# Input product of a recurrent layer in pairs of channel tiles by seven products, on one Trainium2 core

## The chip, the cores and the metric

The kernel runs on one core of one Trainium2 chip, as one program for the whole model. The metric is device time in microseconds (us) for one execution. Its engines are TensorE (PE; PEld is its weight load), VectorE (DVE), ScalarE (ACT), GpSimd (POOL) and SyncE (SP), which issues most DMAs.

## The reference

One sequence of 1024 tokens, model width 1024, two layers, fp32. Layer 0 mixes by retention and a gated delta rule, layer 1 by a gated linear recurrence (RG-LRU); each is followed by a feed-forward block with a short convolution (inner width 2816). The change is about the recurrent mixer of layer 1 and what stands just ahead of it.

```python
h = h + conv_ffn(rms_norm(h, norm_ffn[0]), ...)        # layer 0's feed-forward block
hn = rms_norm(h, norm_mix[1])
h = h + rglru_mixer(hn, ...)                            # layer 1
h = h + conv_ffn(rms_norm(h, norm_ffn[1]), ...)
return rms_norm(h, norm_final)

def rglru_mixer(hn, w_in, conv_w, conv_b, w_a, b_a, w_x, b_x, lam, w_out):
    gate, xr = jnp.split(hn @ w_in, 2, axis=-1)         # w_in: 1024 x 2048, "the input product"
    xr = causal_dwconv(xr, conv_w) + conv_b             # 4 taps along the tokens
    xb = xr.reshape(b, t, 8, 128)                       # 8 channel blocks
    r = sigmoid(einsum('btni,nij->btnj', xb, w_a) + b_a)
    i = sigmoid(einsum('btni,nij->btnj', xb, w_x) + b_x)
    log_a = -8.0 * r * softplus(-lam)
    a = exp(log_a)
    u = sqrt(-expm1(2.0 * log_a)) * (i * xr)
    hs = scan over tokens of hs[t] = a[t] * hs[t-1] + u[t]
    return (gelu(gate) * hs) @ w_out                    # "the output product"

def conv_ffn(hn, w_up, conv_w, conv_b, w_down):
    gate, val = split(causal_dwconv(hn @ w_up, conv_w) + conv_b)
    return (silu(gate) * val) @ w_down
```

## The kernel before, in words

**Layout.** Channels lie on the 128 partitions, the 1024 tokens along the free axis, in two halves of 512. The residual stream is eight tiles `H[0..7]` of 128x1024. A product of fp32 quality is three fp32r matmuls (`mm3`, L313 to L315): each operand is split in a high part, rounded by a ScalarE copy, and a low part, the rest, by a VectorE subtraction; high x high, high x low and low x high are added in PSUM.

**Weights** stream from DRAM in quarters of 128x512: SP issues the load into one of seven buffers `raw`, ScalarE casts `whi` (L267), VectorE makes `wlo` (L268). The order of all quarters is written out in `quarter_order`, and `prefetch` issues loads and splits six quarters (`RING`) ahead of the one in use, so that these steps stand between others in ScalarE's and VectorE's order. Engines work in program order each; outside blocks marked `manual_schedule` a scheduler may still move instructions at build time.

**The feed-forward blocks** take their products in *pairs*: two channel tiles (one of the gate, one of the value) are a 2x2 block problem in output tiles and token columns, done by seven products `o` = 0 to 6 in place of eight (`pair_products`). Each product is 4 x 3 matmuls of 128x512. The seven operands are sums and differences of quarters of the normed input, built once (`operand_steps`: scale, `normal`, `sub`, `high`, `low`) and kept in `s1` and `s2`; the seven weight sums are made by VectorE in `load_pair`. The results need sums too (`pair_sums`): ScalarE copies products 0, 1 and 2 from PSUM into buffers `kept`, VectorE adds products 3 to 5 to these into the two buffers `halo`, ScalarE copies product 6 there. PSUM banks are shared by the string `BANK`: products with the same letter accumulate onto one another.

```python
BANK = "ACACABA"
```

So product 2 adds onto the bank in which product 0 stood, product 3 onto that of product 1, and so on: the next product may begin in a bank when the copy or sum that reads the one before has been done.

The operands for the *second* feed-forward block are built beside matmuls that are going on: those of the first token half (`pair_operands`) while the output product of the recurrent layer is at its second half (called from `down_pairs`), those of the second (`late_operands`) inside `pair_halves`, which does the first pair of products in token halves, with VectorE's and ScalarE's order written out.

**The recurrent layer** does not do this. `down_x`, the end of layer 0's feed-forward block, adds each product to `H` and splits the scaled result for both halves into 32 slots of `s1` (`norm_step`, L383 and L384); the norm factor, one per token, is a row `R` that is multiplied in behind each product. Then eight steps: `proj_x` (one channel tile of the x half: 2 token halves x 8 x 3 matmuls, evacuated by VectorE, L373), `stage_x` (convolution, L1051 and L1053, and the split into `xs`, L586 and L587), `stage_g` for the tile before (12 + 12 matmuls with the two gate matrices into PSUM tiles `pc`, then on ScalarE tanh L1070, exp L1075, tanh L1076, square root L1082, between VectorE's products L1081, L1083, L1084 and the scan L1085), and `stage_y` for the tile before that (the gate half of the input product, L1094, GELU on ScalarE, L1095, product with the scan, L1096, store to `y_dram`). The gates' temporaries are eight 128x512 buffers `us`. A change of function on ScalarE between tanh or exp, square root and GELU shows as an ACT_TABLE_LOAD.

After the last step the y tiles are loaded back and split, and `down_pairs(ys, "lru_out", gain)` does the output product, adds it to `H` and builds the next operands.

## Time and profile before

| | |
|---|---|
| time, median of 3 runs | 2153.62 us (2153.57 to 2155.07) |
| the profiled execution: its time / its span | 2152.99 us / 2151.2 us |
| granted TensorE clock | 0.999 |
| PE busy | 2137.9 us, 99% of the span, 10716 matmuls |
| DVE busy | 1693.5 us, 79% |
| ACT busy | 1082.8 us, 50% |
| POOL busy | 98.2 us, 5% |

The span is the time from the first to the last instruction in the trace; an execution's own time is 1.8 us longer. The recurrent layer stands from about 1206 to 1412 us of the span, its output product behind that. The profile below writes groups of instructions as "line, engine, operation, out<-in by the program's names, partitions x elements, count | busy us, mean ns | idle before, and what ended it", and a timeline as "start, length (both us), engine, line, operation". A timeline row with "x2" holds two instructions one behind the other. An instruction's length includes its start and end latency, so neighbours overlap: the distance between two starts (the pitch) is what one more costs its engine. The column of the granted clock (PEclk) is 1.00 at full speed.

### The profile page before, as it was taken

What the parts mean: (1) busy time and instruction counts of PE and PEld (TensorE: products, weight loads), DVE (VectorE), ACT (ScalarE), POOL (GpSimd) and SP (SyncE); (2) the same over time, 40 slices, a digit from 0 to 9 for tenths busy, and PEclk for the clock granted to TensorE, in tenths of its full rate; (3) what the DMA queues carried; (4) which work ended last, traced back from release to release, by engine and by line L of the source; (5) the groups of instructions that cost most, each with busy time, mean ns of one, the idle gap of its engine ahead of it and who ended that gap; (6) DMA issues with size and microseconds to landing.
All of it is one profiled execution on the core that took longest, in us unless ns stands there. A gap on an engine that the chain in (4) does not pass through costs nothing.

```text
span 2151.2 us, 29709 instructions
## 1 busy us (share of the span) xinstructions
PE 2137.9 (99%) x10716; PEld 1783.3 (83%) x10716; DVE 1693.5 (79%) x2565; ACT 1082.8 (50%) x1748; POOL 98.2 (5%) x114
## 2 busy tenths in 40 slices
PE   9999999999999999999999999999999999999998
PEld 7877889888888888888888888888888888888887
DVE  7995676656999889888866787778999889888645
ACT  6444433235665555555324476756655555554321
POOL 0102022300000000000000000000000000000001
PEclk9999999999999999999999999999999999999999
DMA  5354423444145445437636312242354345375542
GB/s 187 92 168 127 134 89 96 166 128 131 55 155 174 146 158 191 156 109 273 230 104 205 87 54 80 70 154 68 119 180 167 143 159 178 118 266 178 181 169 84
DMA packets 205171, 307.98 MB, mean 143 GB/s; under 512 B 29376, under 2 KB 92384, under 8 KB 205024
## 3 DMA queue, kind: packets, MB, share of 16 engines
q1 hardware_dynamic: 197760, 299.60, 41.9%
q10 hardware_dynamic: 6240, 5.97, 0.9%
q8 instruction: 84, 1.38, 0.3%
q0 software_dynamic: 1024, 0.53, 0.1%
q14 instruction: 63, 0.52, 0.1%
HBM read 215.27 MB, written 90.74 MB: 142 GB/s over the span
## 4 chain that ended last, share of the span: by engine, by line
PE 93%; DVE 3%; DMA 1%; issue 1%; SPq 0%; ACT 0%; POOL 0%; POOLq 0%; DVEq 0%; ACTq 0%
PE ps L313 28%; PE ps L314 28%; PE ps L315 28%; PE pc L313 1%; PE pc L314 1%; PE pc L315 1%; DVE l L1333 0%; DVE l L1331 0%; PE pc L483 0%; DMA l<-gc_dram 0%; DVE wlo L268 0%; PE ps L1508 0%; PE pc L1464 0%; PE ps L1606 0%; PE pc L1576 0%
## 5 line engine op out<-in xcount | busy, mean ns | idle before, releaser
L313 PE MATMUL ps<-s,whi 128*128 128x512 f32 (+1 forms) x2704 | 1054.5, 391 | 1.1 <-ACT s L383 0.7
L314 PE MATMUL ps<-s,whi 128*128 128x512 f32 (+1 forms) x2704 | 1047.9, 388 | 0.5 <-DVE s L900 0.5
L315 PE MATMUL ps<-s,wlo 128*128 128x512 f32 (+1 forms) x2704 | 1047.3, 388 | 0.0
L267 ACT CAST whi<-raw 128x512 fp32r<-128x512 f32 (+1 forms) x620 | 376.6, 613 | 628.4 <-PE ps L314 494.6
L313 PEld LDWEIGHTS ps<-s,whi 128*128 128x128 f32 x2704 | 507.8, 188 | 106.6 <-ACT s L383 1.3
L315 PEld LDWEIGHTS ps<-s,wlo 128*128 128x128 f32 x2704 | 507.7, 188 | 104.7 <-DVE wlo L268 0.6
L314 PEld LDWEIGHTS ps<-s,whi 128*128 128x128 f32 x2704 | 508.1, 188 | 102.5 <-DVE s L900 1.9
L268 DVE TENSOR_TENSOR wlo<-raw,whi 128x512 fp32r<-128x512 f32 (+1 forms) x620 | 415.7, 676 | 72.0 <-ACT whi L267 60.8
L828 DVE SCALAR_TENSOR_TENSOR t<-halo,cols,t 128x1024 f32<-128x1024 f32 x176 | 221.6, 1281 | 2.6 <-ACT t L826 1.6
L801 DVE TENSOR_TENSOR halo<-ps,kept 128x512 f32<-128x512 f32 (+1 forms) x138 | 91.8, 666 | 74.4 <-PE ps L315 73.2
L811 DVE TENSOR_TENSOR h<-ps,h 128x512 f32<-128x512 f32 x112 | 77.3, 690 | 78.8 <-PE ps L315 78.8
L826 ACT ACTIVATE t<-halo,cols 128x1024 f32<-128x1024 f32 x88 | 109.5, 1246 | 18.6 <-DVE halo L801 10.2
L796 ACT COPY kept<-ps 128x512 f32<-128x512 f32 (+1 forms) x138 | 77.1, 558 | 11.0 <-PE ps L315 9.5
L533 DVE TENSOR_TENSOR h<-ps,h 128x512 f32<-128x512 f32 (+1 forms) x72 | 45.2, 630 | 42.4 <-PE ps L315 42.3
L916 DVE TENSOR_TENSOR t<-t 128x1024 f32<-128x1024 f32 x44 | 53.6, 1219 | 0.0
L911 ACT ACTIVATE t<-t 128x1024 f32<-128x1024 f32 x44 | 46.7, 1062 | 10.5 <-DVE t L828 10.5
L852 ACT CAST t<-t 128x512 fp32r<-128x512 f32 x56 | 34.0, 621 | 35.3 <-DVE t L916 33.2
L401 ACT ACTIVATE t<-h 128x512 f32<-128x512 f32 (+1 forms) x49 | 27.3, 562 | 43.6 <-DVE h L533 43.6
L313 PE MATMUL ps<-s,s 128*128 128x256 f32 (+1 forms) x144 | 46.0, 320 | 0.0
L314 PE MATMUL ps<-s,s 128*128 128x256 f32 (+1 forms) x144 | 45.8, 318 | 0.0
L315 PE MATMUL ps<-s,s 128*128 128x256 f32 (+1 forms) x144 | 45.8, 318 | 0.0
L857 DVE TENSOR_TENSOR t<-t 128x512 f32<-128x512 f32 x64 | 43.9, 685 | 0.7 <-DMA sf_dram<-t 0.6
(339 smaller groups left out, 2124.5 us busy)
## 6 DMA issues: line engine op xcount, KB each, us to landing
raw<-in_ffn_up_dram SPq DMA_DIRECT2D x176, 256.0 KB, 2.7
s<-pf_dram SPq DMA_DIRECT2D x112, 256.0 KB, 5.3
sf_dram<-t SPq DMA_DIRECT2D x72, 256.0 KB, 2.5
raw<-in_ffn_w_dram SPq DMA_DIRECT2D x64, 256.0 KB, 2.9
t<-sf_dram SPq DMA_DIRECT2D x58, 256.0 KB, 4.5
pf_dram<-t SPq DMA_DIRECT2D x56, 256.0 KB, 2.6
pf_dram<-lo SPq DMA_DIRECT2D x56, 256.0 KB, 2.5
raw<-in_mix_in_dram SPq DMA_DIRECT2D x52, 256.0 KB, 2.9
```

The lines of the kernel that those rows point to most:

```text
L267: self.nc.scalar.copy(hi[:, 0:w], raw[:, 0:w])
L268: eng.tensor_tensor(lo[:, 0:w], raw[:, 0:w], f32(hi[:, 0:w]), ALU.subtract)
L313: mm(ps, whi, xhi, start=start, stop=False)
L314: mm(ps, whi, xlo, start=False, stop=False)
L315: mm(ps, wlo, xhi, start=False, stop=stop)
L796: A.copy(kept[o], ps)
L801: V.tensor_tensor(dst(i, j), v(ps), v(kept[k]), ALU.add)
L811: V.tensor_tensor(h(*to[o]), ps.rearrange("p (h c) -> p h c", c=256), h(*to[o]), ALU.add)
L826: A.activation(t, buf[:, 2:2 + T], AF.Identity, scale=w(0), bias=self.col(f"ffn_cb{layer}", tile_i))
L828: V.scalar_tensor_tensor(t, buf[:, 2 + j:2 + j + T], w(j), t, ALU.mult, ALU.add)
L911: A.activation(tg, tg, AF.Silu)
L916: V.tensor_tensor(tg, tg, tv, ALU.mult)
```

## The change

The input product of the recurrent layer is done as the feed-forward blocks' are: its 16 channel tiles are eight pairs, and each is taken by seven products. `quarter_order` now has, for `t` = 0 to 3, the pair of x tiles `("lru_p", 2t)`, the pair of gate tiles `("lru_p", 2t + 1)`, and the gate matrices of the two x tiles ahead of the gate pair's product 6 and after it.

- *The operands* are built behind layer 0's feed-forward block: `down_x` is gone and `ffn` calls `down_pairs`, with the inner length of that last product six channel tiles (`ys` 16 to 21). The first x pair goes through `pair_halves`. So the norm is in the operands and no row `R` is multiplied in behind the products.
- *The residual* `H` is stored by SP to `h_dram` as it is formed (16 stores of 256 KB), because its eight tiles are used in the layer: tiles 0 to 3 hold the split x (`xs` before), tiles 4 to 7 the gates' temporaries (`us` before). It comes back in eight loads of 512 KB behind the last pair, four at once and four after 26 more matmul groups.
- *The stages* come in pairs of tiles: x pair, `stage_x` twice, gate pair with `stage_g` after its products 5 and 6, then `stage_y`: two GELUs of 128x1024 from the `halo` buffers, the product with the scan, the store. The scan is written over `x`.
- *The low parts of the weights* are subtracted by GpSimd instead of VectorE from the end of the first x pair to the last x pair (`lo_engine`).
- *The small constants* (softplus and the like, 128x8) lie in a tile `few` that was unused before.
- *The y tiles* 0 to 5 are loaded back between products of the last gate pair, into `s2`, which is now open throughout; tiles 6 and 7 go to `s1`.
- The three matmuls of `mm3` are L316 to L318, the cast and subtraction L269 and L270 in the changed kernel.

```diff
-                for i in range(8):
-                    o.append((("lru_in", 8 + i), 2))
-                    if i >= 1:
-                        o.append((("lru_g", i - 1), 1))
-                    if i >= 2:
-                        o.append((("lru_in", i - 2), 2))
-                o += [(("lru_g", 7), 1), (("lru_in", 6), 2), (("lru_in", 7), 2)]
+                for t in range(4):
+                    o.append((("lru_p", 2 * t), 7))
+                    o += [(("lru_p", 2 * t + 1), range(6)), (("lru_g", 2 * t), 1)]
+                    o += [(("lru_p", 2 * t + 1), range(6, 7)), (("lru_g", 2 * t + 1), 1)]
...
 
+    def rows(self, key):
+        src = self.I["lru_in" if key[0] == "lru_p" else key[0]]
...
+        t, gate = divmod(key[1], 2)
+        first = 2 * t + (0 if gate else 8)
+        return src[first], src[first + 1]
...
-        s = lambda raw: self.split_quarter(raw, V, place=self.extra.pop(len(self.loaded), None))
+        s = lambda raw: self.split_quarter(raw, self.lo_engine, place=self.extra.pop(len(self.loaded), None))
...
-    def down_x(self, ys, name, gain):
...
+    def down_pairs(self, ys, name, gain, groups=None, keep=None):
 
         def then(n, st, m, h):
+            if keep is not None:
+                self.nc.sync.dma_start(keep[m][:, n * HALF:(n + 1) * HALF], h)
...
-            self.down_x(last, f"ffn_d{layer}", gain)
+            self.h_dram = self.tc.dram_tile([KT, P, T], F32, name="h_dram")
+            self.down_pairs(last, f"ffn_d{layer}", gain, lambda n: self.groups(1), self.h_dram)
...
     def rglru(self, gain):
+        H = [self.h_tile(m, F32R if m < 4 else F32) for m in range(KT)]
...
-            return us[:, nu[0] * HALF:(nu[0] + 1) * HALF]
+            return H[4 + nu[0] // 2][:, nu[0] % 2 * HALF:(nu[0] % 2 + 1) * HALF]
...
-            xh, xl = (xs[:, (2 * (i % 2) + j) * T:(2 * (i % 2) + j + 1) * T] for j in range(2))
+            xh, xl = (H[2 * (i % 2) + j] for j in range(2))
...
-            hi, lo = self.quarter(("lru_g", i))
+            hi, lo = self.quarter(("lru_g", i), 0, self.hold)
...
+        def stage_y(t):
+            for i in (2 * t, 2 * t + 1):
+                g = gs[i] = self.R if i % 2 == 0 else f32(self.parts.tile([P, T], F32R, tag="lo", name="lo"))
+                A.activation(g, self.halo[i % 2][:, 4:4 + T], AF.Gelu_apprx_tanh)
+            for i in (2 * t, 2 * t + 1):
+                V.tensor_tensor(gs[i], gs[i], xr.pop(i)[0], ALU.mult)
+                if i < 6:
+                    nc.sync.dma_start(self.y_dram[i], gs[i])
+
+        ys = {}
+
+        def load_y(*ks):
+            for k in ks:
+                ys[k] = self.load_split(self.y_dram[k], self.place2(k))
+
+        def then(t, o):
+            if o >= 5:
+                stage_g(2 * t + o - 5)
+            if t == 3 and o in (1, 2, 4):
+                load_y(*{1: (0, 1), 2: (2, 3), 4: (4, 5)}[o])
+
+        pair = lambda s: ("lru_p", s)
+        with self.tc.manual_schedule(engines={mybir.EngineType.PE}):
+            second = self.pair_products(pair(1), partial(then, 0))
+            self.pair_halves(pair(0), pair(1), second)
+            self.lo_engine = nc.gpsimd
+            stage_x(0)
+            stage_x(1)
+            self.run(second)
+        for t in range(4):
+            if t:
+                self.run(self.pair_products(pair(2 * t)))
+                stage_x(2 * t)
+                stage_x(2 * t + 1)
+                if t == 3:
+                    self.lo_engine = V
+                self.run(self.pair_products(pair(2 * t + 1), partial(then, t)))
+            stage_y(t)
+        H = self.H = [self.h_tile(m) for m in range(KT)]
+        for m in range(4):
+            nc.sync.dma_start(H[m], self.h_dram[m])
+        for i in (6, 7):
+            ys[i] = self.split(gs[i], self.place1(i - 6))
+        self.after(26, lambda: [nc.sync.dma_start(H[m], self.h_dram[m]) for m in range(4, KT)])
+        self.down_pairs([ys[i] for i in range(KT)], "lru_out", gain)
```

Three places show what now stands in an engine's order. ScalarE around the end of a gate chain, in the middle of the layer, before: `pc` are the PSUM tiles of the gates, `us` the temporaries, `ba`, `bx`, `sp`, `spm` the constants.

```order
L1070 ACTIVATE us<-pc,ba 128x512
L1070 ACTIVATE us<-pc,bx 128x512
L1075 ACTIVATE us<-us,spm_10748 128x512 x2
L1076 ACTIVATE us<-us,sp_10746 128x512 x2
L1082 ACT_TABLE_LOAD
L1082 ACTIVATE us<-us 128x512
L586 CAST xs<-t 128x1024
L1082 ACTIVATE us<-us 128x512
L267 CAST whi<-raw 128x512
L1095 ACT_TABLE_LOAD
L1095 ACTIVATE us<-us 128x512
L267 CAST whi<-raw 128x512 x2
```

The same engine in the changed kernel, at the end of the second pass's gates; `h_10744` to `h_10747` are the tiles 4 to 7 that hold the temporaries, `few` the constants, `ps` a PSUM bank of the next x pair.

```order
L1052 ACTIVATE h_10747<-pc,few 128x512
L1056 ACTIVATE h_10747<-h_10745,few 128x512
L1056 ACTIVATE h_10744<-h_10746,few 128x512
L1057 ACTIVATE h_10745<-h_10745,few 128x512
L1057 ACTIVATE h_10746<-h_10746,few 128x512
L1063 ACT_TABLE_LOAD
L1063 ACTIVATE h_10745<-h_10745 128x512
L1063 ACTIVATE h_10746<-h_10746 128x512
L1071 ACT_TABLE_LOAD
L1071 ACTIVATE lo<-halo_99 128x1024
L269 CAST whi<-raw 128x512
L786 COPY kept<-ps 128x512
```

Weight casts and the split of the next tile stood between the steps of one tile's chain; now the chain of the second tile of a pair goes through, the GELU of a whole tile follows it, and the `kept` copy of the next pair's first product comes behind both.

VectorE at the entry of the recurrent layer, before, at the last two channel tiles of the feed-forward output product (`s` slots of `s1`, `t` the squares):

```order
L384 SCALAR_TENSOR_TENSOR s_96<-h_94,cols,s_96 128x512
L405 TENSOR_TENSOR t<-t 128x512
L268 TENSOR_TENSOR wlo<-raw,whi 128x256
L533 TENSOR_TENSOR h_95<-ps,h_95 128x512
L1024 TENSOR_SCALAR nl<-cols 128x8
L1031 TENSOR_SCALAR ba<-cols 128x8
L1032 TENSOR_SCALAR bx<-cols 128x8
L1127 TENSOR_SCALAR sple<-nl 128x8
L1139 TENSOR_SCALAR sp<-nl 128x8
L268 TENSOR_TENSOR wlo<-raw,whi 128x512
L384 SCALAR_TENSOR_TENSOR s_96<-h_95,cols,s_96 128x512
L405 TENSOR_TENSOR t<-t 128x512
```

VectorE at the same place in the changed kernel, up to the transpose (L467) from which the second half's norm row is made (`lo` the second half of an extra weight buffer):

```order
L408 TENSOR_TENSOR halo_99<-halo_99 128x512
L292 TENSOR_TENSOR raw<-raw 128x512
L270 TENSOR_TENSOR wlo<-raw,whi 128x512
L408 TENSOR_TENSOR halo_99<-halo_99,halo_98 128x512
L270 TENSOR_TENSOR wlo<-raw,whi 128x512
L306 TENSOR_TENSOR raw<-raw 128x512
L293 TENSOR_TENSOR raw<-raw 128x512
L536 TENSOR_TENSOR h_95<-ps,h_95 128x512
L270 TENSOR_TENSOR wlo<-raw,whi 128x512 x3
L270 TENSOR_TENSOR lo<-raw,lo 128x512
L291 TENSOR_TENSOR raw<-raw 128x512
L467 STREAM_TRANSPOSE halo_99<-pc 128x128
```

The small constants have left this place and so has the split of the normed input (L384); weight subtractions and the sums of two pairs' weights (L291 to L293, L306) have come ahead of the transpose.

TensorE in the middle of the layer, before, with numbers: the last gate matmuls of one tile (`pc`, operand `xs`) and the first of the input product that follows (`ps`, operand `s1`).

```order
L315 MATMUL pc_11040<-xs_10712,wlo_10836 128x512
L313 MATMUL pc_11045<-xs_10712,whi_10835 128x512
L314 MATMUL pc_11045<-xs_10712,whi_10835 128x512
L315 MATMUL pc_11045<-xs_10712,wlo_10836 128x512
L313 MATMUL ps_11070<-s1_96,whi_10907 128x512
L314 MATMUL ps_11070<-s1_96,whi_10907 128x512
L315 MATMUL ps_11070<-s1_96,wlo_10908 128x512
L313 MATMUL ps_11070<-s1_96,whi_10907 128x512
```

TensorE in the changed kernel, at the start of an x pair; `ps_11683` is the bank of the pair's products 0 and 2, `ps_11702` that of product 1, `ps_11786` the bank of a later product of the pair, whose first matmul the scheduler has put here.

```order
L316 MATMUL ps_11702<-s2_4166,whi_11558 128x512
L317 MATMUL ps_11702<-s2_4166,whi_11558 128x512
L318 MATMUL ps_11702<-s2_4166,wlo_11559 128x512
L316 MATMUL ps_11786<-s1_96,whi_11679 128x512
L316 MATMUL ps_11683<-s2_4166,whi_11577 128x512
L317 MATMUL ps_11683<-s2_4166,whi_11577 128x512
L318 MATMUL ps_11683<-s2_4166,wlo_11578 128x512
L316 MATMUL ps_11683<-s2_4166,whi_11577 128x512
```

Before, a new product began in a PSUM bank of its own; now product 2 (from the second row of `ps_11683` on) adds onto the bank that product 0 filled and that a `kept` copy reads.

More of the change, by code (lines that the diff above doesn't have):

```diff
@@ L129, in __init__ @@
         pad(self.perm, 49, "pad1")
-        self.H = [self.perm.tile([P, T], F32, name=f"h{m}") for m in range(KT)]
+        self.H = [self.h_tile(m) for m in range(KT)]
         self.s1 = self.perm.tile([P, 2, 32, 256], F32R, name="s1")
@@ L211, in quarter_order @@
                 o += [x for _ in range(2) for x in out("ffn_d0", 1)]
-        return [(key, j) for key, n in o for j in range(n)]
+        return [(key, j) for key, n in o for j in (range(n) if isinstance(n, int) else n)]
     @staticmethod
@@ L699, with pair_products @@
     BANK = "ACACABA"
-    def pair_products(self, layer, p, then=None):
-        key = (f"ffn_up{layer}", p)
+    def pair_products(self, key, then=None):
         sums, banks = self.pair_sums(), {}
@@ L709, in pair_products, with pair_halves @@
             yield
-    def pair_halves(self, layer, p, following):
-        key = (f"ffn_up{layer}", p)
+    def pair_halves(self, key, after, following):
         first = self.qpos
@@ L722, in pair_halves @@
         self.prefetch(first)
-        up = self.I[key[0]]
         self.eager = True
-        pair = self.pairs[key[0], p + 1] = self.load_pair(up[p + 1], up[NPAIR + p + 1])
+        pair = self.pairs[after] = self.load_pair(after)
         next(pair)
@@ L932, in ffn @@
         with self.tc.manual_schedule(engines={mybir.EngineType.PE}):
-            second = self.pair_products(layer, 1, partial(after, 1))
-            self.pair_halves(layer, 0, second)
+            up = lambda p: (f"ffn_up{layer}", p)
+            second = self.pair_products(up(1), partial(after, 1))
+            self.pair_halves(up(0), up(1), second)
             after(0, 5)
@@ L939, in ffn @@
         for p in range(2, NPAIR):
-            self.run(self.pair_products(layer, p, partial(after, p)))
+            self.run(self.pair_products(up(p), partial(after, p)))
             if p < NPAIR - 1:
@@ L1845 @@
     b.ffn(0, "g_mix1")
-    b.s2_stack.close()
     b.rglru("g_ffn1")
```

123 lines of the change are left out of this document (34 added, 89 removed).

## The prediction

> **What bounds the kernel now.** I read the page's first and fourth parts, then a table of stages, then the timelines of TensorE, ScalarE and VectorE around the recurrent layer and around the two places where normed operands are already built for paired products.
>
> ```profile
> PE 2137.9 (99%) x10716; PEld 1783.3 (83%) x10716; DVE 1693.5 (79%) x2565; ACT 1082.8 (50%) x1748; POOL 98.2 (5%) x114
> PE 93%; DVE 3%; DMA 1%; issue 1%; SPq 0%; ACT 0%; POOL 0%; POOLq 0%; DVEq 0%; ACTq 0%
> 1240.00:1280.00 40.00, 40.00 (x178) 33.14 (x177) 32.99 (x43) 29.23 (x41) 0.00 (x0) 1.00 0.19 60
> 1457.00:1499.20 42.20, 42.20 (x210) 35.11 (x210) 39.91 (x53) 28.60 (x51) 0.28 (x1) 1.00 0.23 69
> ```
>
> The columns of the last two rows are the stretch, then busy time of PE, weight load, DVE, ACT and POOL. TensorE never waits in the recurrent layer (first of the two), and hardly in the second half of the layer's output product (second), but there VectorE is at 95%. So a matmul removed is worth its pitch, and a wait that is added costs its length. The pitch, from the first and last of 162 full matmuls and of 46 half-wide ones:
>
> ```profile
> 1179.76 0.39 PE L313 MATMUL ps<-s,whi 128*128 128x512 f32 x1
> ...
> 1216.26 0.39 PE L315 MATMUL ps<-s,wlo 128*128 128x512 f32 x1
> ...
> 1502.21 0.28 PE L315 MATMUL ps<-s,wlo 128*128 128x256 f32 x1
> ...
> 1507.61 0.28 PE L315 MATMUL ps<-s,wlo 128*128 128x256 f32 x1
> 1216.58 0.43 PE L474 MATMUL pc<-t,ones 128*32 128x128 f32 x8
> 1219.79 1.05 PE L483 MATMUL pc<-ident,rtok 128*128 128x128 f32 x8
> 1498.47 0.65 PE L474 MATMUL pc<-halo,ones 128*32 128x128 f32 x16
> 1500.98 1.16 PE L483 MATMUL pc<-ident,rtok 128*128 128x128 f32 x8 [0.25 <-POOL rtok L466]
> ```
>
> 36.50/161 = 0.2267 us, and 5.40/45 = 0.12 us.
>
> **The change part by part.** *TensorE's work.* The input product had 16 channel tiles x 48 = 768 matmuls; it has 8 pairs x 7 products x 12 = 672. 96 x 0.2267 = -21.8. The first pair runs in token halves: 168 x 0.12 = 20.2 instead of 84 x 0.2267 = 19.0, +1.1. Token sums and norm rows of the first half now pass through TensorE (0.43 + 1.05), and the second half sums 16 strips, not 8 (+0.22): +1.7. Together -19.0.
>
> *The constants.* Some 28 VectorE operations on 128x8 move from here to the kernel's start, with one small exponential. Before, they hid behind TensorE; at the start they cost between nothing and their own 28 x 0.165 = 4.6:
>
> ```profile
> L1136 DVE TENSOR_TENSOR splq<-splq,spls 128x8 f32<-128x8 f32 x7 | 1.2, 165 | 0.2
> ```
>
> TensorE has other work at the start too, so I take 1.
>
> *The operands behind the feed-forward layer.* The same build runs today behind the recurrent output product, so its rows price it:
>
> ```profile
> 1459.35 2.35 DVE L626 TENSOR_TENSOR t<-t,pc 128x1024 f32<-128x1024 f32 x2
> 1461.69 1.23 DVE L616 TENSOR_TENSOR s<-t,s 128x1024 fp32r<-128x1024 f32 x1
> 1462.83 0.69 DVE L268 TENSOR_TENSOR wlo<-raw,whi 128x512 fp32r<-128x512 f32 x1
> 1463.43 1.22 DVE L631 TENSOR_TENSOR t<-t 128x1024 f32<-128x1024 f32 x1
> ...
> 1498.36 0.68 DVE L290 TENSOR_TENSOR raw<-raw 128x512 f32<-128x512 f32 x1
> 1499.18 0.32 DVE L464 STREAM_TRANSPOSE halo<-pc 128x128 f32<-128x128 f32 x1
> 1499.61 0.17 DVE L465 TENSOR_SCALAR rtok<-halo 128x4 f32<-128x4 f32 x1
> ...
> 1506.69 0.42 DVE L801 TENSOR_TENSOR halo<-ps,kept 128x256 f32<-128x256 f32 x1
> 1499.92 1.01 POOL L466 TENSOR_TENSOR rtok<-rtok,npow 128x4 f32<-128x4 f32 x1 [42.65 <-DVE rtok L465]
> ```
>
> From the first scaling with the norm row (1459.35) to the last step ahead of the second half's transpose (1498.36) VectorE issues 15 wide steps (pitch 1.14) and 34 narrow ones (0.60): 37.5, and 1.5 idle. TensorE covers it with 165 matmuls and a half-wide product, 37.4 + 1.4 = 38.8: just enough. Behind the feed-forward layer the inner length is six tiles, not eight: from norm row to half-wide product stand 113 matmuls, 25.6 + 1.4 = 27.0. VectorE has 15 wide, 29 narrow and 4 half-narrow steps (0.34, the row of L801 less the 0.08 by which steps overlap) there: 35.9, with 0.6 idle 36.5. Then transpose (0.3), two weight sums that now stand ahead of the scale step (1.2), scale (0.2), GpSimd's power (1.0 and its hand-over): the second norm row comes at 39.3. TensorE, with strips (0.65) and the next product (1.4), is ready at 29.1. Wait: 10.2. Ends: 6, if idle and the two sums vanish and weight steps slip behind; 13, with the other build's idle doubled. What is late next: the h additions, hence the residual stores on SP; the weight loads queued behind those stores are issued some 4 us ahead of need, so I cost them at nothing.
>
> *The gates.* Of each pair's banks, the third product adds onto the bank of the first, so TensorE must wait until ScalarE has copied the first product away. In ScalarE's new order that copy stands behind both gate chains of the pair before and the GELU. The pieces, from one chain of today:
>
> ```profile
> 1275.57 0.69 ACT L1070 ACTIVATE us<-pc,ba 128x512 f32<-128x512 f32 x1
> 1276.14 0.69 ACT L1070 ACTIVATE us<-pc,bx 128x512 f32<-128x512 f32 x1
> 1276.85 1.28 ACT L1075 ACT_TABLE_LOAD   x1
> 1278.14 1.52 ACT L1075 ACTIVATE us<-us,spm 128x512 f32<-128x512 f32 x2
> 1279.57 0.80 ACT L1076 ACTIVATE us<-us,sp 128x512 f32<-128x512 f32 x1
> 1280.28 1.04 ACT L586 CAST xs<-t 128x1024 fp32r<-128x1024 f32 x1
> 1281.21 0.81 ACT L1076 ACTIVATE us<-us,sp 128x512 f32<-128x512 f32 x1
> 1282.04 1.28 ACT L1082 ACT_TABLE_LOAD   x1
> 1283.34 1.16 ACT L1082 ACTIVATE us<-us 128x512 f32<-128x512 f32 x2
> 1284.39 0.60 ACT L267 CAST whi<-raw 128x512 fp32r<-128x512 f32 x1
> L911 ACT ACTIVATE t<-t 128x1024 f32<-128x1024 f32 x44 | 46.7, 1062 | 10.5 <-DVE t L828 10.5
> L796 ACT COPY kept<-ps 128x512 f32<-128x512 f32 (+1 forms) x138 | 77.1, 558 | 11.0 <-PE ps L315 9.5
> ```
>
> From the first gate product to that copy, in the second and third pass: first result 0.9 (three matmuls and the last one's end); 8 first tanh x 0.57 = 4.6; 5 table switches x 1.43 (1278.14 - 1276.14 - 0.57) = 7.2; 4 exp x 0.72 and 4 second tanh x 0.71 = 5.7; 4 roots x 0.53 = 2.1; 3 casts at the root's pitch, 1.6; 2 copies x 0.5 = 1.0; 2 GELUs priced as the 128x1024 activation of L911, 2.1: 25.2. TensorE has 61 matmuls until it needs the copy: 13.8. Wait 11.3. In the first pass ScalarE's order holds 7 switches and 5 casts: 29.1, wait 15.3. Three passes: 37.9. Ends 32 (1.1 us less a switch here and there, GELUs at the pitch) and 43 (casts late). VectorE and the DMAs of these passes are hidden: its 35 us stand in a pass of 55. GpSimd takes over 41 wide subtractions; the nearest row is its 128x512 multiply, so 14 of them a pass make 14 x 1.5 = 21 of 55: nothing.
>
> ```profile
> L1541 POOL TENSOR_TENSOR t<-t,l 128x512 f32<-128x512 f32 x16 | 24.0, 1501 | 113.2 <-DVE l L1540 74.7 <-DMA g_dram<-t 38.6
> ```
>
> *The end of the layer.* The last gate chain is followed by two GELUs, 26.1 by the same prices (6 casts). VectorE then ends scan, product and split of the last tile: from the root's end (22.6) 3 narrow steps (1.8), 2 scans at a pitch of 1.13 (2.3, the row below), 2 wide products (2.3) and 4 narrow splits (2.4), 31.4:
>
> ```profile
> 1286.42 1.22 DVE L1085 TENSOR_TENSOR_SCAN t<-us 128x512 f32<-128x512 f32 x1
> 1287.55 0.67 DVE L268 TENSOR_TENSOR wlo<-raw,whi 128x512 fp32r<-128x512 f32 x1
> ```
>
> TensorE has 100 matmuls ahead of the first that needs it, 22.7. Wait 8.7; ends 4 and 13 (the loads of y, through seven raw buffers). The residual comes back by 8 loads of 512 KB, the last of them ahead of additions that are 27 us off: nothing.
>
> *The clock.* These waits idle TensorE for 7 to 9 us at a time. The end of the trace shows what idling does (PEclk is the column after POOL):
>
> ```profile
> 2142.00:2144.00 2.00, 0.59 (x12) 0.50 (x4) 0.42 (x2) 0.00 (x0) 0.69 (x1) 1.00 0.00 0
> 2144.00:2145.00 1.00, 0.21 (x2) 0.02 (x1) 0.75 (x2) 0.00 (x0) 0.00 (x0) 0.91 0.00 0
> 2145.00:2146.00 1.00, 0.00 (x0) 0.00 (x0) 1.00 (x4) 0.00 (x0) 0.00 (x0) 0.50 0.37 129
> ```
>
> Within 2 us of the last matmul the granted clock is at half. How long it takes to return no row shows. I bound it by nothing and by a whole product (12 x 0.2267 = 2.7 lost) behind each of five long waits, and take half: 7, ends 0 and 14. The Trainium skill (TensorE: Matmul & The Clock Gate, Part 1: The HAM clock gate) says that the array falls to half rate after an idle window of about 3.4 us and is back after about as much sustained work; the fall agrees with the row, and its return would make an estimated 1.7 a wait, 8.5 in all instead of 7.
>
> Sum: -19.0 + 1 + 10.2 + 37.9 + 8.7 + 7 = +45.8 on the profiled execution's 2152.99 (span 2151.2), so 2198.8; the median of the runs is 0.6 above that execution, so by this 2198 to 2199.
>
> **The rivals.** *Faster: the copies slip through.* If ScalarE were ahead of TensorE at each gate, as it is in the feed-forward pairs (the row of L796 shows 9.5 us of it waiting for TensorE over 138 copies), only -19.0 + 1 would be left: 2135. For it: ScalarE has work for some 38 of 55 us a pass. Against: the order, not the load, holds the copy. It decides if the chains take under 13.8 instead of 25. 0.07.
>
> *No change: the chains hide but the build does not*: -19.0 + 1 + 10.2 + 8.7 = 2154. 0.03.
>
> *The switch costs twice.* If a table switch took its load once more (1.28 x 22 switches, all on chains: +28), 2227. The Trainium skill (ScalarE: Activation LUTs, What ACT_TABLE_LOAD costs) speaks for this: 1.28 and a drain of 1.38, 2.66 in all for each switch. Against it stand the rows, where from one activation's issue to the next over a switch it is 1.43 beyond the first's pitch, so the old pipeline's end is nearly all that is added. 0.03.
>
> *GpSimd becomes the bound*: if its subtraction, beside VectorE, took over 3.9 us, a pass would stretch with it; at 4.5, 14 x 4.5 = 63 against 55, three times: 2223. The slowest row of its kind says 1.5. 0.04.
>
> **How the numbers follow.** The forecast has 0.83: 2198. Its own range, from the ends: -19 + 6 + 32 + 4 = +23 to -19 + 13 + 43 + 13 + 14 + 4.6 = +69, so 2176 to 2221. What lies beyond (2135, 2154, 2223 and up) holds under 0.2, so the range is 2174 to 2221. A measurement tells 0.2%, 4.3 us, from no change: faster 0.07, same 0.03, slower 0.90.
>
> **What would show it.** 96 fewer matmuls at the same pitch; TensorE idle before the third product of the second, third and fourth x pairs, 7 to 9 us each, put down to the ScalarE copy; idle at the second norm row, put down to GpSimd or VectorE, about 10 in all with the strips; about 9 at the output product's fifth or later operand; the granted clock under 1.00 in those stretches. The prediction is wrong if TensorE's waits in this layer sum to under 25 us, or if its idle time lies elsewhere.

## The result, and the profile after

The changed kernel takes 2213.56 us (median of 4 runs, 2210.54 to 2215.42) against 2153.60 for the kernel before on the same chip: 1.0276 times as long, interval 1.0258 to 1.0294. The forecast was 2198. The profiled execution took 2215.42, its span 2213.6, so 62.4 us more span than before. First the page's busy times (share of the span, count):

```profile
PE 2146.6 (97%) x10728; PEld 1784.9 (81%) x10728; DVE 1742.6 (79%) x2574; ACT 1126.5 (51%) x1828; POOL 168.2 (8%) x156
```

TensorE's busy time rose by 8.7 although its matmuls at full pitch are worth 19.0 less: 27.7 us of busy time came in beyond that. (The count rises by 12 because 84 full matmuls became 168 half-wide ones, and 24 rows of strips and norm came in.) Its idle time, span less busy, rose from 13.3 to 67.0, by 53.7. The waits of TensorE, as line, waited-for engine and line: total us, times, longest:

```profile
PE ps L316 <- ACT whi L269: 23.0, 4, 6.8
PE ps L316 <- ACT h L1052: 10.6, 4, 6.4
PE pc L486 <- POOL rtok L469: 5.3, 3, 2.3
PE pc L316 <- DVE halo L791: 3.5, 2, 1.7
PE pc L477 <- ACT halo L404: 3.1, 1, 3.1
PE pc L316 <- ACT halo L788: 2.7, 2, 1.4
PE pc L477 <- DVE halo L408: 2.4, 1, 2.4
```

Two stretches in the gate passes, around the waits, and one at the layer's end, to be held against the two full rows of before; columns as there (busy PE, PEld, DVE, ACT, POOL, then the granted clock):

```profile
1280.00:1300.00 20.00, 8.30 (x24) 5.71 (x22) 13.55 (x18) 19.84 (x27) 3.21 (x3) 0.77 0.09 27
1340.00:1360.00 20.00, 10.46 (x36) 7.41 (x35) 14.47 (x17) 18.77 (x27) 3.61 (x3) 0.80 0.10 40
1470.00:1486.00 16.00, 11.43 (x37) 7.77 (x36) 12.68 (x19) 13.81 (x20) 0.00 (x0) 0.79 0.55 187
```

Where TensorE was busy without a gap, it now works 8 to 10 of 20 us in these stretches, and ScalarE is the full engine (19.84 of 20). What happens in the first of these stretches, TensorE's timeline (the number in brackets is the idle time before a row):

```profile
1281.95 0.39 PE L318 MATMUL ps<-s,wlo 128*128 128x512 f32 x1
1288.72 0.80 PE L316 MATMUL ps<-s,whi 128*128 128x512 f32 x1 [6.37 <-ACT h L1052]
...
1293.58 0.63 PE L318 MATMUL ps<-s,wlo 128*128 128x512 f32 x1
1299.53 1.28 PE L316 MATMUL ps<-s,whi 128*128 128x512 f32 x2 [5.33 <-ACT whi L269]
1300.61 0.63 PE L317 MATMUL ps<-s,whi 128*128 128x512 f32 x1
1301.04 0.63 PE L318 MATMUL ps<-s,wlo 128*128 128x512 f32 x1
...
1304.40 0.39 PE L317 MATMUL ps<-s,whi 128*128 128x512 f32 x1
1304.63 0.40 PE L318 MATMUL ps<-s,wlo 128*128 128x512 f32 x1
```

and ScalarE's in the same stretch:

```profile
1286.68 1.28 ACT L1052 ACT_TABLE_LOAD   x1
1287.98 2.42 ACT L1052 ACTIVATE h<-pc,few 128x512 f32<-128x512 f32 x4
1290.27 1.53 ACT L1056 ACTIVATE h<-h,few 128x512 f32<-128x512 f32 x2
1291.68 1.52 ACT L1057 ACTIVATE h<-h,few 128x512 f32<-128x512 f32 x2
1293.21 1.28 ACT L1063 ACT_TABLE_LOAD   x1
1294.51 1.15 ACT L1063 ACTIVATE h<-h 128x512 f32<-128x512 f32 x2
1295.68 1.28 ACT L1071 ACT_TABLE_LOAD   x1
1296.97 1.06 ACT L1071 ACTIVATE R<-halo 128x1024 f32<-128x1024 f32 x1
1297.93 1.04 ACT L1071 ACTIVATE lo<-halo 128x1024 f32<-128x1024 f32 x1
1298.88 0.60 ACT L269 CAST whi<-raw 128x512 fp32r<-128x512 f32 x1
1299.39 0.57 ACT L786 COPY kept<-ps 128x512 f32<-128x512 f32 x1
```

TensorE waits twice in one chain: for a PSUM bank that still holds gate results until the second tile's first tanh (L1052) frees it, and then until a weight cast (L269) and the `kept` copy (L786), which stand behind chain and GELUs, are through. From the first tanh of a pass to that copy ScalarE takes 27.2, 26.5 and 26.5 us in the three passes. And behind each of these waits the matmuls run cold, at a pitch of 0.43 instead of 0.23, 7 to 13 of them; at 1304.40 the pitch is full again, 4.9 us after the restart.

The 62.4 us, by place: the idle time is 3.8 at the kernel's start, 7.1 at the layer's entry, 36.5 in the gate passes (13.7, 11.3, 11.5) and 6.6 at the end (54.0; elsewhere it is 0.3 less than before). Of the 27.7, rows with the doubled pitch show 20.9: start 2.1, entry 3.5, passes 4.7, 3.1 and 4.1, end 3.4. Of the other 6.8 some 5 are no slower clock. A matmul just ahead of a gap counts with its whole length (0.39 in the rows above) and not with its pitch: 31 of the 128x512 and 128x256 ones stand ahead of a gap here, 13.0 us in all where their pitches make 6.5; before there were 7, 2.5 against 1.4. A second profiled execution with the same matmuls (`e12_no_residual` below) has 2142.8 busy, so 23.9 in place of 27.7.

### The profile page after: what moved, and what is told of

The parts are those of the page before. It is cut to its first block, busy times and chain, and to the rows that moved or that the text cites. A ratio compares the mean times of both kernels' runs of the same rounds, so it can differ in the third digit from the quotient of the medians.

```text
span 2213.6 us, 29964 instructions
## 1 busy us (share of the span) xinstructions
PE 2146.6 (97%) x10728; PEld 1784.9 (81%) x10728; DVE 1742.6 (79%) x2574; ACT 1126.5 (51%) x1828; POOL 168.2 (8%) x156
## 5 line engine op out<-in xcount | busy, mean ns | idle before, releaser
L316 PE MATMUL ps<-s,whi 128*128 128x512 f32 (+1 forms) x2668 | 1048.0, 394 | 34.3 <-ACT whi L269 23.0
L318 PE MATMUL ps<-s,wlo 128*128 128x512 f32 (+1 forms) x2668 | 1037.3, 389 | 0.1
L269 ACT CAST whi<-raw 128x512 fp32r<-128x512 f32 (+1 forms) x643 | 390.9, 613 | 622.4 <-PE ps L317 496.0
L316 PEld LDWEIGHTS ps<-s,whi 128*128 128x128 f32 x2668 | 506.2, 190 | 142.9 <-ACT whi L269 25.5
L318 PEld LDWEIGHTS ps<-s,wlo 128*128 128x128 f32 x2668 | 505.2, 189 | 104.3 <-DVE wlo L270 1.5
L270 DVE TENSOR_TENSOR wlo<-raw,whi 128x512 fp32r<-128x512 f32 (+1 forms) x597 | 401.4, 678 | 65.4 <-ACT whi L269 54.4
L791 DVE TENSOR_TENSOR halo<-ps,kept 128x512 f32<-128x512 f32 (+1 forms) x165 | 108.6, 659 | 88.2 <-PE ps L318 87.3
L786 ACT COPY kept<-ps 128x512 f32<-128x512 f32 (+1 forms) x165 | 91.3, 553 | 17.1 <-PE ps L318 14.9
L469 POOL TENSOR_TENSOR rtok<-rtok,npow 128x4 f32<-128x4 f32 (+1 forms) x10 | 9.9, 993 | 961.2 <-PE ps L316 608.6
L270 POOL TENSOR_TENSOR wlo<-raw,whi 128x512 fp32r<-128x512 f32 (+1 forms) x46 | 70.8, 1554 | 130.8 <-ACT whi L269 130.8
L605 ACT CAST s<-t 128x1024 fp32r<-128x1024 f32 x39 | 40.9, 1051 | 34.0 <-DVE t L677 18.3
L306 DVE TENSOR_TENSOR raw<-raw 128x512 f32<-128x512 f32 x68 | 50.0, 735 | 6.8 <-POOL wlo L270 6.3
L906 DVE TENSOR_TENSOR t<-t 128x1024 f32<-128x1024 f32 x44 | 53.7, 1220 | 0.0
L292 DVE TENSOR_TENSOR raw<-raw 128x512 f32<-128x512 f32 x68 | 49.8, 733 | 0.3
```

The lines of the kernel that those rows point to most:

```text
L269: self.nc.scalar.copy(hi[:, 0:w], raw[:, 0:w])
L270: eng.tensor_tensor(lo[:, 0:w], raw[:, 0:w], f32(hi[:, 0:w]), ALU.subtract)
L306: V.tensor_tensor(sum1, a12, sum2, ALU.subtract)
L316: mm(ps, whi, xhi, start=start, stop=False)
L318: mm(ps, wlo, xhi, start=False, stop=stop)
L786: A.copy(kept[o], ps)
```

## The experiments

All are edits of the changed kernel, timed beside the kernel before. The theory: the time is lost where ScalarE's chain of gates holds TensorE, plus smaller losses at the start, the entry and the end, each made dearer by the slow clock behind a wait. The rivals put the loss elsewhere: GpSimd, shared PSUM banks, the table switches' price, the residual's way through DRAM.

**The constants late.** The changed kernel's `lru_consts` are the small operations on 128x8; here they are issued behind the 11th pair of layer 0's feed-forward block.

```diff
-            V.tensor_tensor(tg, tg, tv, ALU.mult)
+            mul = V.tensor_tensor(tg, tg, tv, ALU.mult)
+            if layer == 0 and p == 10:
+                with self.tc.issue_after(mul.ins):
+                    self.lru_consts()
```

> The small constants are issued behind the eleventh pair of the first feed-forward block instead of at the kernel's start; nothing else is changed. Theory: at the start they cost 6.9 us, not by their own length but because VectorE's order there has changed and one step of the first norm row (L468) stands behind the second half's squares; then the first norm row comes 6.7 us earlier again and the time is 2206 to 2208. Rival 1: only their own length counts, 28 x 0.165 = 4.6 at most: 2209 or more. Rival 2: the start's delay is absorbed later: 2213.

2210.05 us, ratio 1.0261 (1.0246 to 1.0276): 3.5 less in the median, 4.8 in the span. By the time alone this is the first rival's range (2209 or more), not the theory's; the rows tell the two apart. VectorE's step that the first norm row of the kernel waits for, and that norm row on TensorE, in the changed kernel:

```profile
28.02 0.16 DVE L468 TENSOR_SCALAR rtok<-t 128x4 f32<-128x4 f32 x1
29.83 1.16 PE L486 MATMUL pc<-ident,rtok 128*128 128x128 f32 x8 [2.34 <-POOL rtok L469]
```

and with the constants late:

```profile
20.51 0.17 DVE L468 TENSOR_SCALAR rtok<-t 128x4 f32<-128x4 f32 x1
23.60 1.05 PE L486 MATMUL pc<-ident,rtok 128*128 128x128 f32 x8
```

The constants' own 28 small steps are not what delayed the norm row. With them in place the build-time scheduler put L468 behind seven 128x512 scalings and five squares of the second half (20.17 to 28.02), and TensorE ran dry and went cold.

**The weights' low parts on VectorE.** The line `self.lo_engine = nc.gpsimd` is left out.

```diff
             self.pair_halves(pair(0), pair(1), second)
-            self.lo_engine = nc.gpsimd
             stage_x(0)
```

> The low parts of the weights are subtracted by VectorE throughout; GpSimd does none. Theory (ScalarE's order sets the waits): GpSimd's 41 subtractions are hidden and VectorE has room in the passes, so the time stays within 5 us of 2213.6, and TensorE's waits behind the gates stay 6 to 12 us a pass. Rival (GpSimd delays: its subtractions come late, and VectorE's instructions beside them are stretched, a scan from 1.2 to 2.3 us): 2200 or less.

2203.99, ratio 1.0232 (1.0215 to 1.0249): 9.6 less, more than the theory allowed and less than the rival had. Groups of VectorE's work by line in the gate passes (count, busy, mean ns of one, idle before), in the changed kernel:

```profile
L1066 DVE TENSOR_TENSOR_SCAN t<-h,t,h 128x512 f32<-128x512 f32 x6 | 11.3, 1881 | 0.1
L1065 DVE SCALAR_TENSOR_TENSOR h<-h,h 128x512 f32<-128x512 f32 x12 | 12.1, 1044 | 0.1
L791 DVE TENSOR_TENSOR halo<-ps,kept 128x512 f32<-128x512 f32 x18 | 12.2, 686 | 11.0 <-PE ps L318 11.0
```

and with VectorE subtracting itself:

```profile
L270 DVE TENSOR_TENSOR wlo<-raw,whi 128x512 fp32r<-128x512 f32 x45 | 30.3, 681 | 2.3 <-ACT whi L269 2.2
L1066 DVE TENSOR_TENSOR_SCAN t<-h,t,h 128x512 f32<-128x512 f32 x6 | 7.7, 1279 | 0.1
L1065 DVE SCALAR_TENSOR_TENSOR h<-h,h 128x512 f32<-128x512 f32 x12 | 7.8, 685 | 0.1
L791 DVE TENSOR_TENSOR halo<-ps,kept 128x512 f32<-128x512 f32 x18 | 12.4, 687 | 12.0 <-PE ps L318 12.0
```

The same scan is 602 ns longer on average beside GpSimd, the same product 359 ns, while the sum L791, which has one input in PSUM, is not longer at all. The Trainium skill (SBUF — State Buffer, Who interferes with whom) has the rule for it: VectorE's second read port in SBUF is the one that GpSimd uses, and the two lock each other out. The rows agree. Over the passes, the longer steps (each group's count by the difference of its two means, summed) cost VectorE about 27 us, and the 41 subtractions it was spared are some 28 of the 30.3 us of L270: almost nothing gained. From tanh to `kept` copy the second and third pass take 23.4 us instead of 26.5; the first stays at 27.2. In the 23.4 ScalarE waits for nothing. In the 26.5 it waits three times for VectorE: 1.7 us ahead of a GELU for a sum (L791), and 0.7 and 0.4 for scans (L1066). That sum stood behind a sum of weights (L306), for which VectorE had itself waited 1.2 us until GpSimd was done with a subtraction, and which then took 1.75 us instead of 0.69. So GpSimd costs in two ways: it lengthens the steps beside it, and it comes late.

**One table.** The exponential, the root and the GELU of the layer are all replaced by tanh, so ScalarE never switches there.

```diff
-                A.activation(a, th[n, 0], AF.Exp, scale=spm4[:, i:i + 1], bias=spm4[:, i:i + 1])
+                A.activation(a, th[n, 0], AF.Tanh, scale=spm4[:, i:i + 1], bias=spm4[:, i:i + 1])
...
-                A.activation(sq, sq, AF.Sqrt)
+                A.activation(sq, sq, AF.Tanh)
...
-                A.activation(g, self.halo[i % 2][:, 4:4 + T], AF.Gelu_apprx_tanh)
+                A.activation(g, self.halo[i % 2][:, 4:4 + T], AF.Tanh)
```

> In the recurrent layer exponential, square root and GELU are replaced by tanh, so that ScalarE changes no table there (22 switches fewer); the values of the layer are others. Theory: a switch is worth 1.43 us on the chain, so the chain of a pass shortens by 7 to 10 us, TensorE's waits in the passes and at the end fall from 43 to about 15, and of the 22 us lost to the slow clock about half goes: 2165 to 2185. If a switch costs twice that: 2155 or less. Rival (banks or GpSimd hold TensorE): 2205 or more.

2190.93, ratio 1.0174 (1.0159 to 1.0189): 22.6 less, short of what was expected. The chain fell to 21.2, 20.9 and 20.9 us, so the five switches of the second and third pass are worth 5.6 there, 1.1 each, less than the forecast's 1.43 because ScalarE now waits 1.4 us more for VectorE's scan; without the waits in both they are worth 1.4 each. The rival of a doubled price falls: 22 switches at 2.66 would have been 58.5.

**Banks apart.** The layer's pairs take their PSUM banks from the pool that the gates do not use.

```diff
-            banks[bank] = self.pp(both=True)[:, 0:HALF if n is None else 256]
+            banks[bank] = self.pp(both=self.both)[:, 0:HALF if n is None else 256]
...
+            self.both = False
```

> The pairs of the recurrent layer take PSUM banks of the one group only and the gates have the other four to themselves; before, the two shared all eight. Theory: the wait for a bank that the gates hold (10.6 us over four passes) only moves to the next product, which needs the copy of product 0; what goes is the gates' wait for the pair's banks, 3.1 us in two passes, and a little clock: 2203 to 2212. Rival (shared banks are the cause): the waits for the gates' reader and for the pair's banks go, 17 us, and 8 or more of slow clock: 2188 or less.

2213.72, ratio 1.0280 (1.0265 to 1.0295): no change. TensorE's waits (lines stand one lower here):

```profile
PE ps L317 <- ACT whi L270: 45.8, 5, 14.5
```

The wait on the first tanh is gone, and so are those on L791 and L788; the other is as much longer: one wait of some 14 us in a pass in place of two to four. The bank only decided where in the chain TensorE stood still.

**The chain in blocks.** Exponentials and second tanhs of both tiles are taken together ahead of the next x pair's product 0, the roots together at product 2. This is written for 3 table loads a pass instead of 5 to 7; the trace has 3 in the first pass and 6 in the second and third, 19 in the layer instead of 22, because the scheduler put a GELU and exponentials between the first tanhs. TensorE's order is kept as written.

```diff
+        def rest(t, o):
+            if o == 0:
+                stage_e(2 * t)
+                stage_e(2 * t + 1)
+            if o == 2:
+                stage_s(2 * t)
+                stage_s(2 * t + 1)
...
-                self.run(self.pair_products(pair(2 * t)))
+                    self.run(self.pair_products(pair(2 * t), partial(rest, t - 1)))
```

> The gate chain of a pass is cut in pieces: both tiles' first tanh and the GELUs behind the gate products, exponentials and second tanh of both tiles behind the next x pair's product 0, roots and scans behind its product 2, with the exponentials' outputs where the split x stood; so the copies of products 0 to 2 come between the pieces, and the table changes 3 times a pass and not 5 to 7. GpSimd's subtractions and the shared PSUM banks stay. TensorE's order in the layer is as written. Theory (ScalarE's order holds the copies): a pass goes from 59 us to about 48, 2175 to 2185. Rival (ScalarE's and VectorE's load, not its order, sets the pass): 2200 or more.

2223.06, ratio 1.0321 (1.0305 to 1.0336): slower by 9.5, where some 30 us of gain had been expected. TensorE's waits:

```profile
PE ps L316 <- DVE halo L791: 14.4, 3, 5.0
PE ps L316 <- ACT kept L786: 14.0, 5, 4.4
```

Product 0's copy now goes early, but a block of seven or eight activations stands ahead of product 1's copy, and VectorE's products with the roots stand ahead of the sums of the next pair.

**Blocks with the other three edits.** Constants late, low parts on VectorE, banks apart, and the blocks.

> The cut chain, VectorE for all low parts, the gates' PSUM banks apart, and the constants behind the eleventh pair of the feed-forward layer. Theory: besides the 30 us and more of the cut chain, 4 for the constants and 8 for GpSimd: 2160 to 2172; what is left over the kernel before is the entry (10 with its slow clock) and the end of the layer (9). Rival: without GpSimd VectorE has 41 of the 43.5 us of a pass to do and becomes the bound: above 2175.

2211.44, ratio 1.0267 (1.0252 to 1.0283); the wait for VectorE's sum grew instead of vanishing:

```profile
PE ps L317 <- DVE halo L792: 22.2, 3, 7.7
PE ps L317 <- ACT kept L787: 12.8, 6, 4.3
```

So GpSimd and banks were not what spoiled the blocks: constants late and VectorE alone, without blocks, take 2199.75 (below). The layer has 16 table loads here, four a pass. Fewer switches do not help when a block stands between a product and the step that frees its bank.

**GpSimd at the entry.** The weights' low parts go to GpSimd while the operands of the layer are being built, to take load from VectorE, which has no gap there.

```diff
+            self.lo_engine = nc.gpsimd
             self.down_pairs(last, f"ffn_d{layer}", gain, lambda n: self.groups(1), self.h_dram)
```

> GpSimd subtracts the low parts of the weights also while the operands are built behind the feed-forward layer, where VectorE is busy all the time and TensorE waits 7 us for the second norm row. Theory of the prediction (VectorE's own steps are what is too long; 16 of them, 8 us, go): the wait goes, with 3 us of slow clock: 2203 to 2206. Rival (a subtraction of GpSimd stretches a VectorE step beside it by 1.1 us and takes 0.6 from VectorE): no gain, 2211 to 2220.

2214.72, ratio 1.0287 (1.0270 to 1.0305): nothing gained. The first of the three entry waits, 2.4 before, became

```profile
1225.54 0.66 PE L477 MATMUL pc<-halo,ones 128*32 128x128 f32 x8 [6.82 <-DVE halo L408]
```

while the second fell from 3.1 to 0.7 and the third stayed at 1.6. The rival, that VectorE loses beside GpSimd what it is spared, holds here too: L624, a 128x1024 step, takes 1755 ns on average there instead of 1219, and the step that ends the first wait (L408) stands behind one that waited 1.2 us for a GpSimd subtraction (L306).

**TensorE kept warm.** On top of the banks apart, 52 matmuls into a bank that is overwritten afterwards are put ahead of product 2, in the stretch in which TensorE waits. TensorE's order in the layer is kept as written, which the run with banks apart did not do.

```diff
+            if o == 2 and key in (("lru_p", 2), ("lru_p", 4), ("lru_p", 6)):
+                banks["B"] = self.pp(both=self.both)[:, 0:HALF]
+                x = self.operand(0)
+                for _ in range(52):
+                    self.nc.tensor.matmul(banks["B"], x[:, 0, 0, 0:P], x[:, :, 0, :], start=True, stop=True, skip_group_check=True)
```

> As the run with banks apart (one wait of 14 us ahead of product 2 in three passes), with 52 matmuls ahead of that product that write a bank not yet in use and are never read: 11.8 us of the 14. TensorE's order in the layer is as written. Theory (the clock falls when TensorE idles and each restart then costs 2 to 2.6 us): the matmuls behind the three waits run at a pitch of 0.23 at once, and the time falls by 5 to 8: 2206 to 2209. Rival (the slow pitch there comes from something else, such as the engines beside it): 2213 or more.

2214.20, ratio 1.0283 (1.0268 to 1.0298). The restart in the second pass, with banks apart only:

```profile
1357.38 1.28 PE L317 MATMUL ps<-s,whi 128*128 128x512 f32 x2 [13.80 <-ACT whi L270]
1358.46 0.63 PE L318 MATMUL ps<-s,whi 128*128 128x512 f32 x1
1358.89 0.63 PE L319 MATMUL ps<-s,wlo 128*128 128x512 f32 x1
```

and with the filling matmuls:

```profile
1358.63 0.50 PE L317 MATMUL ps<-s,whi 128*128 128x512 f32 x1 [2.54 <-ACT kept L792]
1358.97 0.39 PE L318 MATMUL ps<-s,whi 128*128 128x512 f32 x1
1359.20 0.39 PE L319 MATMUL ps<-s,wlo 128*128 128x512 f32 x1
```

So idleness is what makes the clock fall: kept busy up to the last 2.5 us, the array starts at full pitch, in the third pass too. In the first pass, where 3.19 us of waiting were left, the pitch falls to 0.43 some 1 us after the restart. But the time did not follow. From the second norm row at the entry to the one behind the output product the trace is 1.5 us shorter, where 5 to 8 were expected. The three restarts lose 1.7 us in slow rows instead of 6.7, but the two at the layer's end, where nothing was filled in, lose 5.8 instead of 4.2; where the rest went is open.

**The chain piece by piece.** On top of constants late, low parts on VectorE and banks apart, `chain` gives out one ScalarE step at a time behind the GELUs, all roots behind the last tanh. `self.steps` puts its pieces between the groups of three matmuls that follow (slots): the first two slots on, then one a slot. TensorE's order is kept as written.

```diff
+        def chain(t):
...
+                    with self.tc.issue_after(last[0].ins):
+                        A.activation(a, th[n, 0], AF.Exp, scale=spm4[:, i:i + 1], bias=spm4[:, i:i + 1])
+                    yield
...
+                gelu(t)
+                if t < 3:
+                    self.steps(2, chain(t))
```

> As the mended run before (cut chain, VectorE for all low parts, banks apart, constants late), but the chain behind the GELUs is given out one ScalarE step per 0.7 us of TensorE's work over the next x pair, exponentials kept behind the GELUs and roots behind the last tanh, so that copies, casts and the sums of the pair come between single steps and not behind blocks of 8. Theory (in-order engines: what counts is what stands ahead of the copies and sums): the waits of 4 and 7 us a pass for a copy and for a sum go, a pass falls from 59 to about 49, 2178 to 2190. Rival (VectorE's and ScalarE's load): no better than 2205.

2200.35, ratio 1.0214 (1.0197 to 1.0231), between theory and rival. Its reference point, constants late and low parts on VectorE with the chain as in the changed kernel, ran with it:

> Only the two small changes: constants behind the eleventh pair of the feed-forward layer, VectorE for all low parts. If the two gains add (3.5 and 9.6): 2199 to 2202.

2199.75, ratio 1.0214 (1.0198 to 1.0229): the two gains add (3.5 + 9.6 = 13.1; measured 13.8), and the fine chain gave nothing on top. The fine chain's waits:

```profile
PE ps L317 <- DVE halo L792: 13.9, 4, 4.5
PE ps L317 <- ACT kept L787: 9.6, 4, 3.3
```

Pieces still stand ahead of copies and sums, and they are written so: three come ahead of product 0's copy (four slots a product, the first piece at the second), and three of the four scans ahead of the sum of product 4, for which product 6 waits. The trace of the second pass has them so: an activation table load, two exponentials and a tanh ahead of the copy at 1334.82, three scans ahead of the sum at 1352.40.

**Copies and sums first.** The same, with the first piece five slots on instead of two, so that product 0's copy is written ahead of it, and with each piece on ScalarE held behind the last `kept` copy written ahead of it, and each on VectorE behind the last sum. The two edits were not run apart.

```diff
-                A.copy(kept[o], ps)
+                self.copied = A.copy(kept[o], ps)
...
-                V.tensor_tensor(dst(i, j), v(ps), v(kept[k]), ALU.add)
+                self.summed = V.tensor_tensor(dst(i, j), v(ps), v(kept[k]), ALU.add)
...
-                    with self.tc.issue_after(last[0].ins):
+                    with self.tc.issue_after(last[0].ins), self.tc.issue_after(self.copied.ins):
                         A.activation(a, th[n, 0], AF.Exp, scale=spm4[:, i:i + 1], bias=spm4[:, i:i + 1])
...
-                    self.steps(2, chain(t))
+                    self.steps(5, chain(t))
```

> As the run with the finely cut chain, but each piece of the chain is kept behind the copy (on ScalarE) and the sum (on VectorE) of the x pair that stands ahead of it as written: copies of products 0, 1, 2 come ahead of the first, fifth and ninth of the eight exponentials and tanh, and the sum of product 3 ahead of all that follows a root. Theory (TensorE waits for what stands ahead of the copy and the sum): the waits of 3.1 and 4.5 us a pass fall below 1, with their slow clock a pass falls from 56 to about 49, 2178 to 2186. Rival (VectorE, with 41 to 45 us of work a pass, is the bound): 2195 or more.

2184.17, ratio 1.0142 (1.0127 to 1.0157), in the theory's range, and 29.4 us under the changed kernel. The waits for copies and sums shrank, but not below 1 each as expected. TensorE's waits:

```profile
PE ps L317 <- ACT whi L270: 7.5, 2, 5.6
PE ps L317 <- ACT kept L787: 7.4, 4, 2.2
PE ps L317 <- DVE halo L792: 6.5, 5, 1.6
```

and one pass, from the start of a pair to the start of the next (columns as above), first in the changed kernel and then here:

```profile
1359.40:1418.38 58.98, 47.52 (x192) 37.75 (x192) 42.30 (x41) 38.87 (x56) 24.29 (x16) 0.91 0.18 58
1287.00:1337.90 50.90, 46.09 (x193) 36.77 (x192) 41.66 (x57) 37.11 (x56) 0.00 (x0) 0.97 0.20 67
```

The 6.5 us of waits for VectorE's sums are spread over five places, the longest 1.6; the clock is at 0.97. It is the best version that was run, and still 30.6 us slower than the kernel before. What stays is the entry, 12.6 us of idle time at the layer's end (the 7.5 above among it) with cold restarts behind it, and some 5 us of waits in each pass (50.90 less 46.09).

**No residual in DRAM.** The 16 stores of `H` are left out and the eight loads read another tensor.

```diff
-            if keep is not None:
-                self.nc.sync.dma_start(keep[m][:, n * HALF:(n + 1) * HALF], h)
...
-            nc.sync.dma_start(H[m], self.h_dram[m])
+            nc.sync.dma_start(H[m], self.y_dram[m])
```

> As the changed kernel without the 16 stores of the residual; the eight loads bring tiles of another buffer of the same size, so the residual is another. Theory (stores and the weight loads queued behind them on SP are hidden): 2211 to 2216, as before within its spread. Rival (the stores delay the first weights and so the entry): 2208 or less.

2214.04, ratio 1.0281 (1.0264 to 1.0298): the stores cost nothing, as forecast. The loads are still there, so this run says nothing of them.

## Why the prediction was right, and where it was not

The direction, the range and the main mechanism held; the time came out 15 us over the forecast. Term by term, the forecast against the two profiled executions:

| step | forecast (ends) | measured |
|---|---|---|
| TensorE's work at full pitch | -19.0 | -19.0 (by the counts) |
| constants at the start | 1 (0 to 4.6) | 3.8 idle, and 2.1 of slow clock |
| wait at the entry | 10.2 (6 to 13) | 7.1 |
| waits in the gate passes | 37.9 (32 to 43) | 36.5 |
| wait at the layer's end | 8.7 (4 to 13) | 6.6 |
| clock | 7 (0 to 14) | 20.9 in rows of doubled pitch, the start's 2.1 in it |
| rest of TensorE's longer busy time | none | 6.8, some 5 of it matmul ends ahead of gaps |
| idle time elsewhere | none | -0.3 |
| sum | 45.8 | 62.4 |

*The gates.* The copy does stand behind both chains and the GELUs, and the chain's length is the loss: it shrank by 3.1 without GpSimd's interference and by 5.6 without switches, and once fewer pieces stood ahead of copies and sums, a pass fell from 59.0 to 50.9 us. The forecast's 25.2 counts from the first gate product to the end of the copy; from the first tanh to the copy's start it is 23.8 (without 0.9 and 0.5), and 27.7 in the first pass. ScalarE's own steps are that long: 23.4 in `e2_lo_vector`, where none of them waits, and 27.2 in the first pass. The other 3.1 of the 26.5 are waits for VectorE, which the forecast didn't have. So the total of 36.5 agrees with 37.9 partly by luck. Behind the chain TensorE was idle 11.7, 8.2 and 8.4, not 15.3, 11.3 and 11.3: its cold matmuls ahead of the copy took twice their time, and in the second and third pass 3.1 us of waiting came earlier. There the gates' own matmuls waited for PSUM banks that a sum and a copy of the gate pair (L791, L788) still read; in the first pass the gates waited 2.0 for the split (L579, L580). These 8.2 us in all the forecast didn't have. It also put the whole wait on the third product, where the trace has two, the first on a bank that a tanh frees; `e4_banks_apart` shows that this split changes nothing. Nor does the forecast agree with itself here: its sum has 15.3 and 11.3 us a pass, its part on the clock and its list of signs 7 to 9; ahead of the third product the trace has 5.3, 6.6 and 6.8.

*The clock is the term that failed.* It was taken as half a product behind each of five long waits. The rows of doubled pitch show 1.5 to 2.7 lost behind each restart in the passes and 3.4 at the end, not 1.35, and some ten restarts, since two waits stand in each pass and the short ones of the entry (2.4, 3.1 and 1.6) make the array cold too. Ten at about 2 are the 20.9. So even the upper end, five full products, was too low: the number of waits was taken from the terms of the sum, each as one piece.

*The constants* cost 3.8 us of idle time and 2.1 of slow matmuls, more than the upper end of 4.6, and not by their own length: with 28 steps more at the start the scheduler moved the step L468 behind the second half's scalings, and `e1_consts_late` takes most of that back. The order of VectorE at the start shows the move without a run; I read that order only around the layer.

*GpSimd* was costed at nothing, from its own load (POOL is busy for 23.6 us of a 57 us stretch in the passes). `e2_lo_vector` prices it at 9.6 us, by the VectorE steps that it lengthens and those that wait for it. In the sum above this is contained in the waits of the passes, so part of the agreement there has a cause that the forecast excluded.

*The entry and the end* came out within their ends, with VectorE almost without a gap ahead of the strips as the forecast had it; 5.5 of the entry's 7.1 us stand at the strips and 1.6 at the norm row. At the end the mechanism was another: 4.2 of the 6.6 are a wait for a weight cast (L269) behind the last GELUs, and 0.3 for the split of the y tiles, on which the forecast had put the whole. The residual's stores are hidden, as it said. The y loads are not quite: ScalarE waits 3.2 us for them in the last pass, and a tanh (L1052) that stands behind their casts holds TensorE for 1.0 of the 6.6.

*The rivals.* The copies did not slip through, no stretch of them; the switch doesn't cost twice (1.1 to 1.4 each, not 2.66); GpSimd did not become the bound, it slowed another engine and made it wait.

## What to carry to other kernels

A saving of matmuls on a TensorE that never waits is worth its pitch only while the step that frees each PSUM bank stays ahead of long chains in its engine's order: here 19 us saved cost some 80, and putting copies and sums ahead of a chain in pieces gave back some 16 of what was lost (2200.35 to 2184.17). When waits are added, count the restarts, not only the idle time: each cost about 2 us of slow matmuls here. And small steps added where an order is made at build time can move a critical one, so the order is to be read at every place where something was added.

## What the hardware showed that I had not expected

The clock falls after short waits too: after 2.43 and 3.08 us of idle time at the entry with 0.4 us of work between them, and after 1.37 and 1.56 us in the second pass with 1.0 us of work between them, the matmuls run at half rate. It comes back after 3.1 to 5.6 us of matmuls, which agrees with the fall and return that the Trainium skill (TensorE: Matmul & The Clock Gate, Part 1: The HAM clock gate) describes, except that single waits here are shorter than its idle window.

A GpSimd subtraction of 1.57 us that reads two SBUF operands lengthened two-operand VectorE steps beside it (scan 1.28 to 1.88 us on average), and left those with a PSUM operand alone (0.686 against 0.687, and 0.68 for the four that ran wholly beside one).
